# Hybrid encoder layer: gated output stored as VectorE's 32x32 blocks lie and placed at the loads; last step's loads in another order

## The chip, the core and the metric

One core of one Trainium2 chip runs the whole program. The metric is the device time in microseconds (us) of one execution. The engines are TensorE (PE; its weight loads are listed as PEld), VectorE (DVE), ScalarE (ACT), GpSimd (POOL) and SyncE (SP), which issues most of the transfers. Each engine runs its own instructions in order; between engines a semaphore makes one wait for another. All data are float32; matmuls that matter are split into a high and a low part, and three products of the parts are summed.

## The reference

One encoder layer on x (1, 2048, 1024). The input projection feeds two groups of heads; their outputs are joined and go through one output projection, with a residual and a layer norm:

```python
def hybrid_mixer(x, ...):
    (g_q, g_k, g_v, g_gate, g_lr_f, g_lr_b, m_cq, m_ckv, m_kr, m_gate) = jnp.split(x @ w_in, idx, axis=-1)
    o_a = gla_branch(...)   # (1, 2048, 512)
    o_b = mla_branch(...)   # (1, 2048, 512)
    return jnp.concatenate([o_a, o_b], axis=-1) @ w_out
# gla_branch ends:
    o = rms_norm(o_fwd + o_bwd, norm_g).reshape(B, S, D_GLA)
    return o * jax.nn.silu(gate)
# the layer:  x <- LayerNorm(alpha * x + hybrid_mixer(x))
```

`gla_branch` is a gated linear attention with 4 heads, forward and backward; `mla_branch` is a dense softmax attention with 4 heads and a gate. The change concerns the gated output of the first group, `o_a`, on its way to the output projection.

## The kernel before

The 2048 positions are 16 chunks of 128. The program has these stages, with their approximate place in the profiled execution:

- First sweep (0 to 340 us): the projections of the gated linear attention, chunk by chunk from the last. Each chunk's decayed queries, the intra-chunk output, the state and the gate go to scratch in DRAM (`qd_s`, `oi_s`, `su_s`, `u_s`).
- Second sweep (340 to 585 us): 16 chunks in 8 steps of 2. It loads a chunk's four scratch tensors, makes PE's product of queries and state (`Ob`), adds the intra-chunk output (`oib`), normalizes and gates (`og`), transposes on VectorE (`oT`) and stores the result to `oa_s`. In the same steps it does the projections of the second group: `ipm`, its norm `rm`, `cqT`, `pqr`, and the rope parts `qrTh`, `qrTl`, stored to `rh_s`, `rl_s`.
- Attention (580 to 1115 us): 16 blocks of a head and 512 queries. The first output chunks' loads are issued in its last blocks.
- Output projection (to the end): 16 chunks, each 48 matmuls, then residual and layer norm on VectorE, then two stores.

The order of the second sweep is written out as a table: `PLACE_C` gives each piece of work two places (for the first and the second chunk of a step, in units of steps), `PLACE_C_FIRST` and `PLACE_C_LAST` replace some of them for the first and the last step, and all pieces are sorted by place and then issued. `lS`, `lq`, `lo`, `lu` are the loads of `SU`, `qdb`, `oib` and `ub`; `lx` that of x. All of them are issued by SP, through `gl_load`, into tiles with two buffers each (three for `ub`). A load into a buffer that is in use waits on SP until the reader is done, and everything behind it in SP's order waits too.

`c_oT` (L1491) is VectorE's transpose: it turns each 32x32 block of the 128x512 tile in place and leaves the blocks where they are. A full transpose needs the blocks exchanged as well, within a head: before the change `c_soT` (L1493 to 1497) does that in the store, by four DMAs of 32 partitions, one for each block column, each in runs of 32 floats (128 bytes). `oa_s` then has the layout that the output projection needs, and `OutProj.load` (L1897) reads a chunk with one DMA, 128 rows of 2 KB.

`load` also fetches the chunk's gates (`gr`, two DMAs) and the second group's output (`of[:, 1]`). `load_res` (L1919) fetches `xr`, the residual of the chunk, 512 KB. In the loop over the chunks 4 to 15, ACT, POOL and SP follow the written order: split the loaded tensors of chunk c+2 into high and low parts, load chunk c+4, load the residual of c+1, product of c, finish of c (layer norm and stores). The loads end with chunk 15, so from the iteration of chunk 12 on there are none. `residual` (L1973) is VectorE's `rr = alpha * xr + product` and `finish` the norm. In between stand the last attention block's closing pieces: `tsum` (PE's `sx`, transposes of the softmax sums), `rcp` (VectorE's `rc`, L1677 and 1678) and `turn` (PE's `rt`, L1689). On PE and VectorE the order of the tail isn't written out but follows from a scheduler.

Of the kernel before, what the change touches and what calls it, by code (L numbers as in the profile page):

```python
# [9 lines left out]
F32 = mybir.dt.float32  # L10
# [8 lines left out]
P = 128  # L19
# [3 lines left out]
NCH = S // P  # L23
H = 4
# [63 lines left out]
    lo=(11.99, 11.22, 11.21, 12.62, 11.98, 11.51, 10.87, 10.63),  # L88
# [21 lines left out]
    lo=(15.35, 16.07, 20.38, 20.41, 24.45, 25.82, 33.5, 36.25),  # L110
# [55 lines left out]
    oT=(0.392, 1.103),  # L166
# [20 lines left out]
    lq=(-0.391, -0.03),  # L187
    lo=(-0.5, 0.357),
# [51 lines left out]
    oT=(0.805, 1.172),  # L240
# [20 lines left out]
    lq=(-1.8, 0.09),  # L261
    lo=(-0.452, -1.813),
# [37 lines left out]
    oT=(0.337, 0.509),  # L300
# [17 lines left out]
    vl=(0.968, 2.242),  # L318
    qrfa=(0.871, 2.029),
    lS=(-0.721, -0.203),  # L320
    lq=(-0.287, -0.357),
    lo=(-0.124, 0.045),
    lu=(0.281, 0.47),
    lx=(-0.48, -0.573),
    soT=(1.09, 2.304),
# [21 lines left out]
class K:  # L347
# [146 lines left out]
    def run(self):  # L494
        tc, nc, ins = self.tc, self.nc, self.ins
        with ExitStack() as top:
            cp = top.enter_context(tc.tile_pool(name="const", bufs=1))
            self.cp = cp
            dp = top.enter_context(tc.tile_pool(name="scr", bufs=1, space=DRAM))
# [4 lines left out]
            self.qa_s = [[dp.tile([P, H, QB], F32, name=f"q{p}_s{b}") for p in "hl"] for b in range(NQB)]  # L504
            self.qr_s = [[dp.tile([H, 64, QB], F32, name=f"r{p}_s{b}") for p in "hl"] for b in range(NQB)]
            self.gm_s = [dp.tile([P, H, QB], F32, name=f"gm_s{b}") for b in range(NQB)]
            self.oa_s = [dp.tile([P, H, P], F32, name=f"oa_s{c}") for c in range(NCH)]
            self.qk_s = [[dp.tile([64, H, P], F32, name=f"{n}_s{c}") for c in range(NCH)] for n in ("qx", "kx")]
            self.kt_s = [dp.tile([P, H, P], F32, name=f"kt_s{c}") for c in range(NCH)]
            self.r_s = [dp.tile([1, H, QB], F32, name=f"r_s{b}") for b in range(NQB)]  # L510
# [103 lines left out]
    def sweep_a(self):  # L614
        tc, nc, ins, cp = self.tc, self.nc, self.ins, self.cp
        with ExitStack() as ctx:
# [73 lines left out]
            def step(i, steps):  # L690

                def after(g, k):
                    for n, d, *count in steps.get((g, k), ()):
                        j = {"prev": i - 1, "cur": i, "next": i + 2}[d]
                        if n == "ld":
                            if j < NCH:
                                next(self.ga_ld(j))
                            elif j == NCH:
                                self.xb = self.load_x(NCH - 1, "xb")
                        elif n == "rope":  # L700
                            next(tables, None)
                        elif count:
                            some(n, j, *count)
                        elif (n, j) in begun:
                            for _ in begun.pop((n, j)):
                                pass
                        else:
                            run(n, j)
                for g in range(3):
                    for k in self.products(ch[i], g, after):  # L710
                        pass
                    after(g, NK - 1)
                if i and ch[i]["c"] not in LATE_GATES:
                    for k in self.gate_products(ch[i]["c"], *ch[i]["x"], ip):
                        after(3, k)
                    self.gate_end(ch[i]["c"], g1)

            self.first_lr = wdone[7][0]
            step(0, {(1, 5): [("lrT", "cur")]})
            ch[1]["x"] = self.split_x(xp, xnext, NCH - 2, "xa", "dve", 2)  # L720
            run("bst", 0)
            self.wgr = [self.wgp.tile([P, 512], F32, tag="wg", name=f"wgr{k}") for k in range(NK)]
            for k, raw in enumerate(self.wgr):
# [28 lines left out]
            with self.in_order(last):  # L752
                run("k", i)
                run("q", i)
# [347 lines left out]
    def late_gates(self):  # L1102
# [24 lines left out]
            self.Wz = next(wz)  # L1127
        self.tail = {e: self.merge(e, names) for e, names in zip(ENGINES[1:], (TAIL_ACT, TAIL_DVE))}

    def split_c(self, xf, j, eng="pool"):  # L1130
        self.hi(self.xch[:, :, j], xf)
        self.lo(self.xcl[:, :, j], xf, self.xch[:, :, j], eng)
# [358 lines left out]
        self.nc.vector.transpose(f2(d["oT"]), f2(d["og"]))  # L1491

    def c_soT(self, d):  # L1493
        t = d["oT"].rearrange("p h (a t) -> p h a t", a=4)
        dst = self.oa_s[d["c"]].rearrange("(a r) h (b t) -> b r h a t", a=4, b=4)
        for b in range(4):
            self.nc.sync.dma_start(dst[b], t[32 * b:32 * b + 32])

    def rope(self, dst, src, c, n):

# [37 lines left out]
    def attention(self):  # L1538
# [4 lines left out]
        with ExitStack() as ctx:  # L1543
# [269 lines left out]
            with fixed():  # L1813
                load(4)
                for c in (2, 3):
                    op.load_res(rest[c])
                load(5)
                split(4)
                load(6)
                op.load_res(rest[4])  # L1820
                for c in (0, 1):
                    op.finish(rest[c])
                split(5)
                load(7)
                op.load_res(rest[5])
                for c in (2, 3):
                    op.residual(rest[c], 0)
                    op.residual(rest[c], 1)
                    op.finish(rest[c])
# [16 lines left out]
class OutProj:  # L1846
# [39 lines left out]
    def load(self, o):  # L1886


        kern, nc, c = self.k, self.nc, o["c"]
        b, cs = c // 4, slice((c % 4) * P, (c % 4 + 1) * P)  # L1890
        of = o["of"] = kern.xfp.tile([P, 2, 4, P], F32, tag="xf", name=f"of{c}")
        if c < 4:
            gr = kern.xfp.tile([P, 2, 4, P], F32, tag="xf", name=f"gr{c}")
        else:
            gr = self.gr[c % 2] = self.gr.get(c % 2) or self.slot(f"gr{c}").rearrange("p a (b d) -> p a b d", b=4)
        o["gr"] = gr
        nc.sync.dma_start(of[:, 0], kern.oa_s[c])  # L1897
        nc.sync.dma_start(gr[:, 0], kern.gm_s[b][:, :, cs])
        nc.sync.dma_start(gr[:, 1], kern.r_s[b][:, :, cs].to_broadcast([P, 4, P]))
        nc.sync.dma_start(of[:, 1], kern.ob_s[b][:, :, cs])  # L1900
        o["oh"], o["ol"] = [], []
# [158 lines left out]
```

## Time and profile before

| | us |
|---|---|
| three runs | 1268.89, 1270.41, 1271.71 |
| median | 1270.41 |
| the profiled execution | 1270.53 |
| its span, first to last instruction | 1268.4 |
| PE busy in the span | 1247.2 (98%) |
| DVE busy | 893.5 (70%) |
| ACT busy | 727.9 (57%) |
| POOL busy | 718.6 (57%) |

The profiled execution's time is 2.13 us over its span. The mean granted TensorE clock is 0.997 of full speed. The profile's rows name a line of the kernel, an engine, an operation, and the output and inputs by the program's names. A number in brackets at the end of a row is the idle time just before it, with the engine or DMA that ended it; "us from issue to landing" is the time of a transfer from SP's instruction to its arrival.

### The profile page before, as it was taken

The numbers are of one execution on the slowest core, as the hardware profiler recorded it, in microseconds if no ns is written. First come the engines' busy times: TensorE is split into PE (matmuls) and PEld (weight loads), VectorE is DVE, ScalarE is ACT, GpSimd is POOL, SyncE is SP. The second block draws the span as 40 slices with busy tenths as digits, with TensorE's granted clock in tenths as the row PEclk, the third lists the DMA queues.
The fourth block names the chain that finished last, engine by engine and source line by source line (L and its number), as shares of the span: only waits on it lengthen the run. The fifth ranks groups of instructions, "written<-read, shape, count | busy, mean of one in ns | idle before, by whom it ended". The sixth has DMA issues, their size and how long they took to land.

```text
span 1268.4 us, 19649 instructions
## 1 busy us (share of the span) xinstructions
PE 1247.2 (98%) x6950; PEld 1100.2 (87%) x6950; DVE 893.5 (70%) x1610; ACT 727.9 (57%) x1177; POOL 718.6 (57%) x443
## 2 busy tenths in 40 slices
PE   8999999999999999989999999999999999999997
PEld 7999999999899999988788888888888888887886
DVE  6635555553665545564888888888888888389997
ACT  7544343454665444444888888888888888411110
POOL 0132323223265554430798888889999999935541
PEclk9999999999999999999999999999999999999999
DMA  8224555565857766747211111202133120376662
GB/s 297 76 82 124 136 144 137 144 134 159 274 173 211 210 187 204 211 133 199 76 32 53 40 45 42 59 9 59 58 92 92 42 42 26 122 231 195 208 191 100
DMA packets 188546, 160.10 MB, mean 126 GB/s; under 512 B 97206, under 2 KB 139838, under 8 KB 188448
## 3 DMA queue, kind: packets, MB, share of 16 engines
q1 hardware_dynamic: 180384, 156.72, 43.2%
q0 software_dynamic: 672, 2.10, 0.4%
q8 instruction: 55, 0.90, 0.3%
q10 hardware_dynamic: 7392, 0.03, 0.3%
q14 instruction: 43, 0.35, 0.1%
HBM read 102.79 MB, written 56.00 MB: 125 GB/s over the span
## 4 chain that ended last, share of the span: by engine, by line
PE 87%; issue 3%; DMA 3%; POOL 2%; DVE 2%; ACT 2%; SPq 1%; DVEq 0%; POOLq 0%; ACTq 0%
PE pz L1244 7%; PE ipm L1315 5%; PE o L412 5%; PE o L413 5%; PE o L414 4%; PE pS L1562 4%; PE pS L1563 4%; PE pS L1564 4%; PE pS L1565 4%; PE pS L1566 4%; PE ipa L412 4%; PE ipa L414 4%; PE ipa L413 4%; PE ipg L414 2%; PE ipg L413 2%
## 5 line engine op out<-in xcount | busy, mean ns | idle before, releaser
L364 POOL TENSOR_TENSOR pl<-s,ph 128x1024 fp32r<-128x1024 f32 x128 | 306.7, 2415 | 51.5 <-ACT ph L358 48.0
L1584 DVE TENSOR_TENSOR rm<-pS,rm 128x512 f32<-128x512 f32 x210 | 144.8, 690 | 36.3 <-ACT s L1571 30.7
L1571 ACT ACTIVATE s<-pS 128x1024 f32<-128x1024 f32 x128 | 131.2, 1025 | 61.3 <-PE pS L1566 51.7
L1608 DVE TENSOR_TENSOR s<-s,mb 128x1024 f32<-128x1024 f32 x128 | 151.2, 1213 | 8.9 <-PE mb L1602 8.2
L358 ACT ACTIVATE ph<-s 128x1024 fp32r<-128x1024 f32 x128 | 135.0, 1056 | 17.2 <-PE o L414 16.5
L1612 ACT ACTIVATE s<-s 128x1024 f32<-128x1024 f32 x128 | 131.4, 1049 | 9.4 <-DVE s L1608 9.3
L412 PE MATMUL ipa<-wah,xah 128*128 128x384 f32 (+1 forms) x384 | 128.8, 335 | 5.5 <-ACT wah L358 5.5
L413 PE MATMUL ipa<-wal,xah 128*128 128x384 f32 (+1 forms) x384 | 124.5, 324 | 0.0
L414 PE MATMUL ipa<-wah,xal 128*128 128x384 f32 (+1 forms) x384 | 124.5, 324 | 0.0
L1079 POOL TENSOR_TENSOR Sb<-Sb,Us 64x512 f32<-64x512 f32 x15 | 19.9, 1324 | 169.7 <-DVE Us L1071 160.6
L1562 PE MATMUL pS<-qh,ckvT_h 128*128 128x512 f32 x256 | 102.6, 401 | 0.8 <-DVE rm L1584 0.4
L412 PE MATMUL o<-ph,vh 128*128 128x512 f32 x256 | 101.1, 395 | 0.0
L1563 PE MATMUL pS<-ql,ckvT_h 128*128 128x512 f32 x256 | 100.0, 391 | 0.0
L1564 PE MATMUL pS<-qh,ckvT_l 128*128 128x512 f32 x256 | 99.9, 390 | 0.0
L1565 PE MATMUL pS<-rh,krs 128*128 128x512 f32 x256 | 99.9, 390 | 0.0
L1566 PE MATMUL pS<-rl,krs 128*128 128x512 f32 x256 | 99.8, 390 | 0.0
L414 PE MATMUL o<-ph,vl 128*128 128x512 f32 x256 | 99.8, 390 | 0.0
L413 PE MATMUL o<-pl,vh 128*128 128x512 f32 x256 | 99.7, 389 | 0.0
L1635 DVE TENSOR_TENSOR ap<-ap,s 128x512 f32<-128x512 f32 x120 | 83.0, 692 | 2.7 <-ACT s L1612 0.7
L412 PEld LDWEIGHTS ipa<-wah,xah 128*128 128x128 f32 x384 | 73.1, 190 | 8.4 <-ACT wah L358 5.5
L364 POOL TENSOR_TENSOR ol<-of,oh 128x512 fp32r<-128x512 f32 x32 | 43.0, 1344 | 64.3 <-ACT oh L358 64.3
L413 PEld LDWEIGHTS ipa<-wal,xah 128*128 128x128 f32 x384 | 73.2, 191 | 0.8 <-DVE wal L364 0.2
(302 smaller groups left out, 3427.3 us busy)
## 6 DMA issues: line engine op xcount, KB each, us to landing
xcf<-xT_dram SPq DMA_DIRECT2D x16, 512.0 KB, 5.4
xr<-x_dram SPq DMA_DIRECT2D x16, 512.0 KB, 6.3
out_dram<-rr SPq DMA_DIRECT2D x32, 256.0 KB, 2.1
xaf<-xT_dram SPq DMA_DIRECT2D x14, 512.0 KB, 4.2
oib<-oi_s SPq DMA_DIRECT2D x16, 256.0 KB, 3.7
qdb<-qd_s SPq DMA_DIRECT2D x16, 256.0 KB, 3.5
SU<-su_s SPq DMA_DIRECT2D x16, 256.0 KB, 3.9
ub<-u_s SPq DMA_DIRECT2D x16, 256.0 KB, 3.9
```

The source lines that it names most:

```text
L358: return nc.scalar.activation(dst, src, AF.Copy).ins
L364: return e.tensor_tensor(dst, src, hi.bitcast(F32), ALU.subtract).ins
L412: mm(out, ah, bh, start=start, stop=False)
L413: mm(out, ah, bl, start=False, stop=False)
L414: mm(out, al, bh, start=False, stop=stop)
L1562: mm(ps[:, e], kh, qh, start=True, stop=False)
L1563: mm(ps[:, e], kh, ql, start=False, stop=False)
L1564: mm(ps[:, e], kl, qh, start=False, stop=False)
L1565: mm(ps[:, e], kr, rh, start=False, stop=False)
L1566: mm(ps[:, e], kr, rl, start=False, stop=True)
L1584: V.tensor_tensor(d["rm"], src[:, e], d["rm"], ALU.max)
L1608: V.tensor_tensor(s, s, d["mb"][:, None, :].to_broadcast([P, 2, QB]), ALU.subtract)
```

## The change

Two things change. The gated output is stored by one DMA per chunk, with the 32x32 blocks where VectorE left them (`oa_s` becomes heads x partitions x columns), and the blocks are put in their places when the output projection loads them: four DMAs, one for each 32 partitions of the target, in runs of 128 bytes. And in the last step of the second sweep the places of the loads `lq` and `lo` are others.

```diff
@@ PLACE_C_LAST
     lS=(-0.721, -0.203),
-    lq=(-0.287, -0.357),
-    lo=(-0.124, 0.045),
+    lq=(-0.357, 0.05),
+    lo=(-0.14, 0.045),
     lu=(0.281, 0.47),
@@ scratch
-            self.oa_s = [dp.tile([P, H, P], F32, name=f"oa_s{c}") for c in range(NCH)]
+            self.oa_s = [dp.tile([H, P, P], F32, name=f"oa_s{c}") for c in range(NCH)]
+    def blocks_of(self, src):
+
+        v = src.rearrange("i (b r) m t -> m r (i b) t", b=4)
+        return [(slice(32 * m, 32 * m + 32), v[m]) for m in range(4)]
@@ c_soT
-        t = d["oT"].rearrange("p h (a t) -> p h a t", a=4)
-        dst = self.oa_s[d["c"]].rearrange("(a r) h (b t) -> b r h a t", a=4, b=4)
-        for b in range(4):
-            self.nc.sync.dma_start(dst[b], t[32 * b:32 * b + 32])
+        self.nc.sync.dma_start(self.oa_s[d["c"]].rearrange("h p f -> p h f"), d["oT"])
@@ OutProj.load
-        nc.sync.dma_start(of[:, 0], kern.oa_s[c])
+        for r, src in kern.blocks_of(kern.oa_s[c].rearrange("h p (m t) -> h p m t", t=32)):
+            nc.sync.dma_start(of[r, 0].rearrange("p h (b t) -> p (h b) t", t=32), src)
```

The first place is SP's order in the last step of the second sweep. The number in a name is the chunk (`qdb15` is chunk 15), for `rh`, `rl` the head group and step; the shape is the target's. Before:

```order
L1423 DMA ub13_6552<-u_s13_121 128x512
L1423 DMA qdb15_6555<-qd_s15_75 128x512
L1423 DMA qdb14_6572<-qd_s14_74 128x512
L1423 DMA SU15_6584<-su_s15_107 128x512
L1292 DMA rh_s2_136<-qrTh5_6320 128x256 x2
L1292 DMA rl_s2_137<-qrTl5_6321 128x256 x2
L1423 DMA oib14_6630<-oi_s14_90 128x512
L1423 DMA oib15_6692<-oi_s15_91 128x512
L1497 DMA oa_s12_156<-oT12_6421 128x4x32 x4
```

Now:

```order
L1428 DMA ub13_6516<-u_s13_121 128x512
L1428 DMA qdb14_6519<-qd_s14_74 128x512
L1428 DMA SU15_6546<-su_s15_107 128x512
L1428 DMA oib14_6582<-oi_s14_90 128x512
L1297 DMA rh_s2_136<-qrTh5_6287 128x256 x2
L1297 DMA rl_s2_137<-qrTl5_6288 128x256 x2
L1428 DMA oib15_6654<-oi_s15_91 128x512
L1428 DMA qdb15_6656<-qd_s15_75 128x512
L1499 DMA oa_s12_156<-oT12_6388 128x4x128
```

`qdb14` is now the first of the two, `qdb15` has moved behind `oib15`, `oib14` stands directly behind `SU15` and ahead of the four rope stores, and the store of `oa_s` is one row.

The second place is SP's order in the output projection, around one block of loads (chunk 9's, issued in the iteration of chunk 5; `xr6` is the residual of chunk 6). Before:

```order
L1989 DMA out_dram<-rr4_12056 128x512 x2
L1897 DMA of9_12122<-oa_s9_153 128x512
L1898 DMA gr5_11884<-gm_s2_142 128x4x128
L1899 DMA gr5_11884<-r_s2_210 128x4x128
L1900 DMA of9_12122<-ob_s2_214 128x4x128
L1919 DMA xr6_12127<-x_dram 128x1024
L1989 DMA out_dram<-rr5_12178 128x512 x2
```

Now:

```order
L1992 DMA out_dram<-rr4_12035 128x512 x2
L1900 DMA of9_12101<-oa_s9_153 32x16x32 x4
L1901 DMA gr5_11851<-gm_s2_142 128x4x128
L1902 DMA gr5_11851<-r_s2_210 128x4x128
L1903 DMA of9_12101<-ob_s2_214 128x4x128
L1922 DMA xr6_12109<-x_dram 128x1024
L1992 DMA out_dram<-rr5_12160 128x512 x2
```

The one row of `oa_s` has become four, ahead of the other loads and of `xr6`; the order is otherwise the same.

The third place is VectorE's reciprocal of the last attention block's sums (`rc15`), which the scheduler has moved. Before it stood behind chunk 5's residual:

```order
L1988 TENSOR_SCALAR rr4_12056<-rr4_12056,ln4_r_12094,lnb_11717 128x512 x2
L1973 TENSOR_SCALAR rr5_12178<-xr5_11961,po5_12129 128x512 x2
L1974 BN_STATS bn5_12179<-rr5_12178 128x6 x2
L1677 TENSOR_REDUCE rc15_12209<-sx15_12204 128x4
L1982 BN_AGGR mv5_12184<-bn5_12179 128x2
```

Now it stands in chunk 2's layer norm:

```order
L1986 TENSOR_SCALAR u2_11946<-mv2_11945 128x1
L1988 TENSOR_SCALAR rr2_11939<-rr2_11939,mv2_11945,lng_11680 128x512 x2
L1679 TENSOR_REDUCE rc15_12191<-sx15_12186 128x4
L1680 RECIPROCAL rc15_12191<-rc15_12191 128x4
L431 TENSOR_TENSOR ln2_t_11952<-ln2_y_11954,u2_11946 128x1
```

PE's transposes `sx15` that feed it have moved by about two chunks of matmuls as well. ACT's and POOL's order is the same as before.

## The prediction

> **What bounds the kernel now.** The page's head and its line of busy times come first.
>
> ```profile
> span 1268.4 us, 19649 instructions
> PE 1247.2 (98%) x6950; PEld 1100.2 (87%) x6950; DVE 893.5 (70%) x1610; ACT 727.9 (57%) x1177; POOL 718.6 (57%) x443
> ```
>
> TensorE (PE) is busy for 98% of the span, so a change that leaves its matmuls as they are can win only where PE stands still or runs at a lower clock. The next view, the table by stretches of time, says where that is. Its columns are the length, the busy time of PE, of its weight loads, of VectorE (DVE), ScalarE and GpSimd (POOL), the granted clock, the DMA share and GB/s. The rows are the middle of the second sweep, its last step, and the output projection.
>
> ```profile
> 500.00:540.00 40.00, 40.00 (x299) 39.12 (x299) 18.12 (x63) 18.74 (x49) 18.82 (x20) 1.00 0.68 203
> 540.00:580.00 40.00, 36.78 (x252) 34.45 (x251) 22.17 (x82) 17.27 (x56) 10.13 (x15) 0.96 0.54 147
> 1200.00:1240.00 40.00, 40.00 (x178) 33.12 (x178) 39.03 (x56) 6.25 (x16) 19.59 (x15) 1.00 0.56 178
> ```
>
> In the middle of the sweep PE has no gap. In the last step it loses 3.22 us of 40 and some clock besides. In the output projection PE is full, but DVE is too, at 39.03 of 40: there a delay of DVE has nowhere to go. The change touches just these two places.
>
> The next rows are the same table over 4 us each, with PE alone.
>
> ```profile
> 553.00:557.00 4.00, 1.38 (x6) 0.95 0.81 226
> 557.00:561.00 4.00, 3.71 (x17) 0.63 0.50 102
> ```
>
> Right after PE's longest gap the granted clock is 0.63 for 4 us. The stall costs its own length and then (1 − 0.63) × 4 = 1.48 and (1 − 0.95) × 4 = 0.2: 1.7 us of clock.
>
> The timeline of SyncE's queue (SPq) and its waits show what began that gap: the columns are start, length, line and transfer.
>
> ```profile
> 535.26 9.54 SPq L1423 DMA_DIRECT2D qdb<-qd_s  x2
> 544.89 0.74 SPq L1423 DMA_DIRECT2D SU<-su_s  x1
> 547.62 0.94 SPq L1423 DMA_DIRECT2D oib<-oi_s  x2
> SPq L1423 <- PE Ob L1462: 51.3, 9, 10.3
> ```
>
> SP issues in order. The second of the two qdb loads needs the buffer that PE's Ob of chunk 13 reads; SP stood 10.3 us before it (the last number, the longest of 9 waits). Behind it stand SU(15), four stores of two rope tensors, and only then oib(14), at 547.62. DVE and PE then wait for that transfer:
>
> ```profile
> 547.93 1.05 PE L1462 MATMUL Ob<-SU,qdb 128*128 128x128 f32 x8
> 551.40 0.70 DVE L1465 TENSOR_TENSOR Ob<-Ob,oib 128x512 f32<-128x512 f32 x1 [3.51 <-DMA oib<-oi_s]
> 555.82 0.42 DVE L364 TENSOR_TENSOR qrTl<-tq,qrTh 128x256 fp32r<-128x256 f32 x1
> 556.39 0.39 PE L412 MATMUL pqr<-wqr_h,cqT_h 128*128 128x256 f32 x1 [2.61 <-DVE rm_t L431]
> 557.29 0.58 PE L414 MATMUL pqr<-wqr_h,cqT_l 128*128 128x256 f32 x1 [0.30 <-DVE cqT_l L364]
> PEld pz L1244 <- DVE og L1485: 0.3, 1, 0.3
> ```
>
> DVE waits 3.51 us for oib, everything queued behind it on DVE is late by that, and PE's pqr waits 2.61 and 0.30 us for DVE.
>
> **The last step's loads: what it is worth.** The new order puts qdb(14) first, whose buffer is free early, and holds qdb(15) back to the end. SU(15) still waits for chunk 13's Ob, so SP is released at the same 544.4 (544.89 less the qdb issue of about 0.5). But oib(14) now stands directly behind SU(15): it goes out near 545.2 where it went out at 547.62, 2.4 us earlier. The add at 551.40 could then start at 549.0; PE's Ob(14), which ends at 547.93 + 1.05 = 548.98, is the other thing it needs and allows that too. DVE's chain moves up 2.4 us, so of the gaps of 2.61 and 0.30, about 0.5 stays: −2.4. If the gap is that short I take the clock dip as gone: −1.7. What is late next is the weight load that waits for og, 0.3 us now; I give back 0.2. **Sum −3.9 us.** Bounds: −2.2 if the dip stays, and 0 if SU(15) or a full DMA queue holds oib back as before. What qdb(15) loses by going last is covered: its Ob(15) runs one chunk later.
>
> On that dip the Trainium skill ("TensorE: Matmul & The Clock Gate", section "Part 1: The HAM clock gate (the "warmup" mystery)") says that the array falls to half clock after an idle window of about 3.4 us. Taken to the letter, a gap of 2.61 us would have no dip and the sum would be −2.2; the row with 0.63 shows a dip, and the measurement decides.
>
> **The store by one DMA instead of four.** It takes 48 issues from SP in the sweep:
>
> ```profile
> L1497 SPq DMA_DIRECT2D oa_s<-oT x64: 580/632/1392, 375.9 to 587.0; - x64
> 554.68 2.60 SPq L1497 DMA_DIRECT2D oa_s<-oT  x4
> L1897 SPq DMA_DIRECT2D of<-oa_s x16: 325/384/791, 940.7 to 1221.1; - x16
> ```
>
> Of the four issues' 2.60 us per chunk about 2 go. No engine waits for SP there but for the buffer wait above, and PE is full at 500 to 540, so I cost it at 0. The 0.2 in which the last stores of the step could help later loads is inside the error.
>
> **The load by four DMAs instead of one.** In the output projection each chunk's block of loads now issues four pieces of 32 partitions in 128-byte runs. The nearest row is the store of the same shape (x64 above, 632 ns; four of them 2.60 us) against 0.34 to 0.38 for the single load. So all that SP issues behind it, xr above all (the residual's 512 KB), goes out **δ = 2.60 − 0.34 = 2.3 us** later. From below: four pieces at the shortest issue of the loads, 325 ns, give δ = 1.0. From above: the landing of the small-run stores spreads to 5.5 where the median is 3.2, so the pieces may also hold the queue 2.3 us longer: δ = 4.6. I take 2.3, the row of the same shape.
>
> ```profile
> DMA to landing us min/median/max: 2.2/3.2/5.5
> ```
>
> Is there slack? xr(c+1) is issued behind the load of chunk c+4, which stands behind the stores of chunk c−1's result, which wait for DVE to finish chunk c−1. So a late DVE makes the next xr late, and δ comes on top once per two chunks. The rows are xr's issue with its landing, in the order of chunks 10, 12 and 13 (two more below), then the DVE instruction that needs each of chunks 2, 6, 8, 10, 12.
>
> ```profile
> L1919 SPq DMA_DIRECT2D xr<-x_dram x1: 617/617/617, 1202.1 to 1202.1; - x1
> DMA to landing us min/median/max: 7.2/7.2/7.2
> L1919 SPq DMA_DIRECT2D xr<-x_dram x1: 616/616/616, 1223.3 to 1223.3; - x1
> DMA to landing us min/median/max: 6.6/6.6/6.6
> L1919 SPq DMA_DIRECT2D xr<-x_dram x1: 424/424/424, 1242.3 to 1242.3; - x1
> DMA to landing us min/median/max: 3.6/3.6/3.6
> ```
>
> ```profile
> L1919 SPq DMA_DIRECT2D xr<-x_dram x1: 562/562/562, 1115.7 to 1115.7; - x1
> DMA to landing us min/median/max: 8.1/8.1/8.1
> L1919 SPq DMA_DIRECT2D xr<-x_dram x1: 868/868/868, 1160.7 to 1160.7; - x1
> xr<-x_dram SPq DMA_DIRECT2D x16, 512.0 KB, 6.3
> 1123.89 0.69 DVE L1973 SCALAR_TENSOR_TENSOR rr<-xr,pmb 128x512 f32<-128x512 f32 x1 [2.22 <-POOL of L1906]
> 1168.22 0.68 DVE L1973 SCALAR_TENSOR_TENSOR rr<-xr,pmb 128x512 f32<-128x512 f32 x1
> 1188.58 0.69 DVE L1973 SCALAR_TENSOR_TENSOR rr<-xr,pmb 128x512 f32<-128x512 f32 x1 [0.20 <-DMA xr<-x_dram]
> 1209.82 0.68 DVE L1973 SCALAR_TENSOR_TENSOR rr<-xr,pmb 128x512 f32<-128x512 f32 x1
> 1231.03 0.68 DVE L1973 SCALAR_TENSOR_TENSOR rr<-xr,pmb 128x512 f32<-128x512 f32 x1
> ```
>
> The slack of each is the start on DVE less issue plus landing. Chunk 2: 1123.89 − 1123.8, about 0. Chunk 6 (its landing taken at the page's median, 6.3): 1168.22 − 1167.0 = 1.2. Chunk 8 waits already: 0. Chunk 10: 1209.82 − 1209.3 = 0.5. Chunk 12: 1231.03 − 1229.9 = 1.1. With D as DVE's delay, D grows by 2.3 less the slack each time: 2.3, then 3.4, 5.7, 7.5, 8.7 at chunk 12. From the iteration of chunk 12 on no block is loaded, so xr of 13 to 15 takes no δ. At the end DVE has room, since it waits for PE there:
>
> ```profile
> 1257.53 0.42 DVE L1964 SCALAR_TENSOR_TENSOR rr<-xr,po 128x256 f32<-128x256 f32 x1 [1.46 <-PE po L414]
> 1260.40 0.42 DVE L1964 SCALAR_TENSOR_TENSOR rr<-xr,pap 128x256 f32<-128x256 f32 x1 [2.00 <-PE pap L414]
> ```
>
> That is 3.46 us. **Loss: 8.7 − 3.46 = 5.2 us**; in general 5δ − 2.8 − 3.46, at least 0.
>
> **The sums of the last attention block** move two chunks earlier on PE, and DVE makes their reciprocal earlier. This takes away one wait of PE:
>
> ```profile
> 1160.38 0.27 PE L1689 MATMUL rt<-ident,rc 128*4 128x128 f32 x1 [0.93 <-DVE rc L1677]
> ```
>
> While DVE sets the end, those 0.93 us only lengthen PE's later wait, so it is 0 here, and −0.93 where PE sets the end.
>
> **Sum:** −3.9 + 5.2 = +1.3 on the span of 1268.4: 1269.7. The profiled execution took 1270.53 us, 2.13 more than its span, so it becomes 1271.8. It lies 0.12 above the median of the runs, 1270.41; against that median I say **1271.7 us**. A measurement here can tell about 0.2% (2.5 us) from no change: faster ends at 1267.9, slower begins at 1272.95.
>
> **Rivals.**
> *The backlog swallows the delay (faster).* xr landed in 3.6 us at 1242.3, when no block was loaded, and in 6.6 to 8.1 behind one: most of its time is the queue ahead of it, so a later issue need not land later. With δ = 1.0, D is 1.0, 0.8, 1.8, 2.3, 2.2: under 3.46, no loss. Then PE sets the end, −3.9 − 0.93 = −4.8: 1265.6. Against it: DVE's 0.20 wait at 1188.58 shows xr with nothing to spare. Chance 0.25.
>
> *The small pieces land late (slower).* The 128-byte runs make 2048 packets per block of what were 2-KB rows, in the stretch with a DMA share of 0.56, and xr comes behind them on the same engines. With δ = 4.6: 5 × 4.6 − 6.26 = 16.7, less 3.9: +12.8, 1283.2. It makes the kernel slower by over 0.2% from 5δ − 6.26 − 3.9 = 2.5, δ = 2.5. For it: the spread of the landings of such stores. Against it: their median of 3.2 is no longer than that of larger transfers. Chance 0.28.
>
> The Trainium skill ("DMA: Bandwidth & Descriptors", section "🔬 Bandwidth") speaks for this rival: it calls transfers under 64 KB dominated by descriptors and gives 0.95 us for one of 64 KB. Four would be 3.8 us, an estimate from that page; with about 1 for the single load δ would be 2.9 and the sum +4.3. No run here shows such loads yet.
>
> *The stall stays (slower).* If SU(15) holds oib(14) back as qdb did, or oib lands no earlier through the backlog (DMA share 0.81 at 553), the gain is 0 and 5.2 remain: 1275.6. Chance 0.08.
>
> **How the numbers follow.** The forecast, most of the gain given back and a little more, has 0.39, with a range of its own of 1267.9 to 1274, of which 0.03 lies on the faster side, 0.22 within 0.2%, and 0.14 slower. Faster: 0.25 + 0.03 = 0.28. Same: 0.22. Slower: 0.28 + 0.08 + 0.14 = 0.50. The range reaches to the faster rival, 1265.5, and into the slower one up to 1280, δ = 4 (5 × 4 − 6.26 − 3.9 = 9.8); what is left out is the upper part of it and a gain over 4.9.
>
> **What would show it.** In the changed trace: PE's gap before pqr under 1 us and a clock of 1.00 at 553 to 561 (else the dip is not the gap's); SP's longest wait still before SU(15), with oib(14) right behind it; the four oa_s issues at about 2.6 us per block; DVE waiting for xr at chunks 2, 8 and 10, and less than 1.46 and 2.00 us for PE at the end. It is wrong if DVE waits for xr nowhere, or if ScalarE or POOL waits for the blocks themselves: I price their lateness at 0, since POOL is idle for half of 1200 to 1240 (19.59 of 40) and reads a block two chunks after its load.

## The result, and the profile after

The changed kernel takes 1268.35 us (median of 21 runs, 1266.51 to 1269.89) where the kernel before took 1270.71 (21 runs, 1268.89 to 1272.68). The ratio is 0.9982, with a 95% interval from 0.9976 to 0.9989: 2.4 us faster, just under the 0.2% that I took for the bound of a difference, but clear of no change. I had forecast 1271.7, a little slower. The profiled execution of the changed kernel took 1269.21 us, 0.86 over its median, and that of before 1270.53, 0.18 under its own; so a comparison of the two profiled executions shows 1.3 us of the 2.4.

The page of the changed kernel begins like this, the span and the busy time of each engine:

```profile
span 1267.4 us, 19686 instructions
PE 1246.5 (98%) x6950; PEld 1098.7 (87%) x6950; DVE 889.6 (70%) x1610; ACT 728.2 (57%) x1177; POOL 720.3 (57%) x443
```

The table by stretches (length, then PE, weight loads, DVE, ACT and POOL busy, granted clock, DMA share, GB/s) for the last step of the sweep and the output projection, and behind it the same with PE alone for the 8 us after the stall of before:

```profile
540.00:580.00 40.00, 38.43 (x275) 36.21 (x274) 23.34 (x87) 19.85 (x60) 11.58 (x17) 1.00 0.49 152
1200.00:1240.00 40.00, 40.00 (x178) 33.14 (x177) 37.42 (x53) 5.89 (x15) 17.97 (x14) 1.00 0.62 175
```

```profile
553.00:557.00 4.00, 2.62 (x13) 1.00 0.90 316
557.00:561.00 4.00, 3.85 (x31) 1.00 0.00 0
```

PE's busy time in the last step rises from 36.78 to 38.43 of 40, and the clock, which had averaged 0.63 over those 4 us, is 1.00. SyncE's timeline of that step and the instructions on DVE and PE that had waited:

```profile
535.47 1.16 SPq L1428 DMA_DIRECT2D qdb<-qd_s  x1
544.78 0.32 SPq L1428 DMA_DIRECT2D SU<-su_s  x1
545.14 1.06 SPq L1428 DMA_DIRECT2D oib<-oi_s  x1
549.29 0.70 DVE L1470 TENSOR_TENSOR Ob<-Ob,oib 128x512 f32<-128x512 f32 x1 [1.14 <-PE Ob L1467]
554.28 0.36 PE L412 MATMUL pqr<-wqr_h,cqT_h 128*128 128x256 f32 x1 [0.69 <-DVE rm_t L431]
555.19 0.38 PE L414 MATMUL pqr<-wqr_h,cqT_l 128*128 128x256 f32 x1 [0.44 <-DVE cqT_l L364]
557.15 0.67 PE L1320 MATMUL ipm<-wmh,xcl 128*128 128x448 f32 x2 [0.40 <-POOL xcl L364]
```

oib(14) goes out at 545.14 where it went out at 547.62. DVE's add now waits for PE and no longer for a transfer, and PE's gap before pqr is 0.69 + 0.44 us where it was 2.61 + 0.30. A wait of 0.40 for GpSimd is new.

The output projection has new waits. Rows of PE's, DVE's, SyncE's and GpSimd's timelines:

```profile
1148.91 0.50 PE L412 MATMUL pmb<-woh,oh 128*128 128x512 f32 x1 [0.37 <-ACT oh L358]
1150.78 0.50 PE L414 MATMUL pmb<-woh,ol 128*128 128x512 f32 x1 [1.14 <-POOL ol L364]
1173.08 0.27 PE L1691 MATMUL rt<-ident,rc 128*4 128x128 f32 x1 [1.14 <-ACT rt L1697]
1122.79 0.69 DVE L1976 SCALAR_TENSOR_TENSOR rr<-xr,pmb 128x512 f32<-128x512 f32 x1 [3.18 <-DMA xr<-x_dram]
1200.52 1.28 DVE L1976 SCALAR_TENSOR_TENSOR rr<-xr,po 128x512 f32<-128x512 f32 x2 [1.79 <-DMA xr<-x_dram]
1222.94 1.28 DVE L1976 SCALAR_TENSOR_TENSOR rr<-xr,po 128x512 f32<-128x512 f32 x2 [1.37 <-DMA xr<-x_dram]
1259.39 0.42 DVE L1967 SCALAR_TENSOR_TENSOR rr<-xr,pap 128x256 f32<-128x256 f32 x1 [0.99 <-PE pap L414]
1222.03 2.05 SPq L1900 DMA_DIRECT2D of<-oa_s  x4
1116.22 4.52 SPq L1900 DMA_DIRECT2D of<-oa_s  x4
1130.47 3.15 POOL L1909 TENSOR_TENSOR of<-of,gr 128x512 f32<-128x512 f32 x2 [2.50 <-DMA of<-ob_s]
```

The four pieces take SyncE 1.91 to 2.06 us in 11 of the 16 blocks, and more in the pieces before the loop: 4.52, 3.46 and 2.97 us for chunks 5, 6 and 7, where the single load took 0.57, 0.33 and 0.41. DVE waits for xr at chunk 2 (3.18 us; before, it waited 2.22 there, for GpSimd) and at chunks 9 and 11. GpSimd waits 2.50 us for chunk 5's block itself, which it did not before. DVE's room at the end shrinks from 3.46 to 0.99 us. It is not used up: PE still sets the end. PE itself waits 2.65 us (0.37 + 1.14 + 1.14) in this stage where it waited 1.41.

To place gains and losses I cut each trace at two of PE's instructions that all kernels have. The first is the first `Op` that waits for DVE at the end of the first sweep, the second the first `mx` of the attention, and the end is PE's last matmul. For the two kernels these rows are:

```profile
335.85 1.16 PE L1054 MATMUL Op<-V,At 128*128 128x128 f32 x8 [0.58 <-DVE At L1047]
603.68 0.66 PE L1590 MATMUL mx<-ident,rm 128*128 128x128 f32 x4 [0.31 <-DVE rm L1584]
1260.09 0.28 PE L414 MATMUL pap<-woh,ol 128*128 128x256 f32 x1
```

```profile
336.10 1.16 PE L1054 MATMUL Op<-V,At 128*128 128x128 f32 x8 [0.58 <-DVE At L1047]
601.03 0.66 PE L1592 MATMUL mx<-ident,rm 128*128 128x128 f32 x4 [0.31 <-DVE rm L1586]
1259.07 0.28 PE L414 MATMUL pap<-woh,ol 128*128 128x256 f32 x1
```

The stretch with the last step (A) went from 267.83 to 264.93, a gain of 2.90 us. The rest, with the output projection (B), went from 656.41 to 658.04, a loss of 1.63. The same cuts in all profiled executions, with each kernel's median and its ratio to the kernel before in the same job (95% interval):

| kernel | A | B | median, us | ratio |
|---|---|---|---|---|
| before | 267.83 | 656.41 | 1270.71 | |
| the change | 264.93 | 658.04 | 1268.35 | 0.9982 (0.9976 to 0.9989) |
| e1 places alone | 265.92 | 656.30 | 1268.60 | 0.9981 (0.9972 to 0.9990) |
| e2 layout alone | 269.82 | 656.95 | 1272.76 | 1.0018 (1.0009 to 1.0027) |
| e3 places, load in 4 x 32 rows | 265.55 | 659.52 | 1269.53 | 0.9991 (0.9980 to 1.0002) |
| e4 change, residual first in the loop | 265.02 | 656.27 | 1267.90 | 0.9978 (0.9968 to 0.9987) |
| e5 only lq | 266.95 | 654.73 | 1269.89 | 0.9994 (0.9984 to 1.0003) |
| e6 only lo | 266.45 | 655.62 | 1268.15 | 0.9984 (0.9975 to 0.9993) |
| e7 change, blocks not placed | 264.96 | 655.00 | 1267.17 | 0.9975 (0.9967 to 0.9984) |
| e8 change, residual first everywhere | 264.97 | 655.49 | 1267.22 | 0.9973 (0.9963 to 0.9983) |
| e9 change, 8 pieces | 264.96 | 667.66 | 1279.19 | 1.0067 (1.0050 to 1.0083) |
| e10 change, pieces from ScalarE | 264.94 | 669.11 | 1277.84 | 1.0063 (1.0044 to 1.0082) |
| e11 e1, residual first everywhere | 266.02 | 656.73 | 1269.33 | 0.9988 (0.9979 to 0.9996) |

A is steady: the six profiles that share the change's store and places (the change, e4, e7, e8, e9, e10) lie between 264.93 and 265.02. B is one execution each and less steady: before, e1, e5 and e6 have the same instructions in the same order in the output projection and lie between 654.73 and 656.41. Most of that spread is PE's waits for rc and rt (1.41 us in the kernel before, 1.57 in e1, 0.49 in e6, none to be seen in e5). The kernel before is at the upper end, and the profiled executions of e5 (1268.18) and e10 (1282.18) are the fastest and the slowest run of theirs. So a difference of 1 us or so in B has to be read together with the medians.

The kernels also differ in what the scheduler made of the tail. PE's and VectorE's order in the output projection is that of the kernel before in e1, e5, e6 and e7, and PE's in e3, e10 and e11 too. The earlier sums of the last attention block (`sx`, `rc`, and with them one `rt`) stand in the change and in e2, on PE also in e4 and nearly so in e9; e8 has an order of its own. PE's row of the sums in the change and in e7:

```profile
1123.24 0.60 PE L1673 MATMUL sx<-ident,acc 128*128 128x128 f32 x4
```

```profile
1146.07 0.60 PE L1673 MATMUL sx<-ident,acc 128*128 128x128 f32 x4
```

So a comparison of B across these groups is one of two orders as well as of two ways to load. No run has the change's loads with the order of before on SyncE, PE and VectorE.

### The profile page after: what moved, and what is told of

Same layout as the page of the kernel before. It is cut to its first block, busy times and chain, and to the rows that moved or that the text cites. A ratio compares the mean times of both kernels' runs of the same rounds, so it can differ in the third digit from the quotient of the medians.

```text
span 1267.4 us, 19686 instructions
## 1 busy us (share of the span) xinstructions
PE 1246.5 (98%) x6950; PEld 1098.7 (87%) x6950; DVE 889.6 (70%) x1610; ACT 728.2 (57%) x1177; POOL 720.3 (57%) x443
## 4 chain that ended last, share of the span: by engine, by line
PE 88%; DMA 3%; DVE 2%; issue 2%; ACT 2%; POOL 1%; SPq 1%; DVEq 0%; POOLq 0%; ACTq 0%
PE pz L1249 7%; PE ipm L1320 5%; PE o L412 5%; PE o L413 5%; PE o L414 5%; PE pS L1564 4%; PE pS L1566 4%; PE pS L1567 4%; PE pS L1568 4%; PE pS L1565 4%; PE ipa L412 4%; PE ipa L414 4%; PE ipa L413 4%; PE ipg L414 2%; PE ipg L412 2%; PE ipg L413 2%
```

## The experiments

**e1: the last step's places alone** (kernel before, with the change's two lines of the table).

```diff
-    lq=(-0.287, -0.357),
-    lo=(-0.124, 0.045),
+    lq=(-0.357, 0.05),
+    lo=(-0.14, 0.045),
```

> The kernel before with only the last step's load places of the change; store and loads of oa_s as before. Theory A (the two edits act apart: the last step gains about 2.9 us, the four-piece loads cost 1.2 to 1.6 us in the output projection): this part alone gains the whole 2.9 us or a little more, 1267.2 to 1268.0 beside a before of 1270.7, so it is at least as fast as the change; in the trace PE's gap before pqr is about 1.1 us with a clock of 1.00 at 553 to 561, and DVE's room at the end stays near 3.5 us less what PE came earlier. Theory B (the output projection takes the gain back whatever the loads look like, since VectorE and SyncE there come no earlier when PE does): 1269.0 to 1270, slower than the change, with new PE waits between 1140 and 1180.

Measured: 1268.60, and neither theory as it was put. B shows no loss (656.30), so the output projection does not take the gain back by itself: theory B falls. But A gained only 1.91 us where the change gained 2.90. The trace says why. Its rows on DVE, PE and SyncE:

```profile
557.25 1.13 DVE L1485 SCALAR_TENSOR_TENSOR og<-Ob,rg_r,ub 128x128 f32<-128x128 f32 x4 [1.23 <-DMA ub<-u_s]
564.45 0.39 PE L1244 MATMUL pz<-xch,wzh 128*128 128x256 f32 x1 [0.90 <-DVE og L1485]
549.31 2.73 SPq L1497 DMA_DIRECT2D oa_s<-oT  x4
552.78 0.62 SPq L1423 DMA_DIRECT2D ub<-u_s  x1
```

With oib(14) early, the next in line is the gate tensor ub: its load stands behind the four store DMAs of chunk 12 and goes out at 552.78; DVE waits 1.23 us for it and PE 0.90 for DVE. In the changed kernel the store is one DMA, ub goes out at 550.30, and both waits are gone:

```profile
549.21 0.48 SPq L1499 DMA_DIRECT2D oa_s<-oT  x1
550.30 0.73 SPq L1428 DMA_DIRECT2D ub<-u_s  x1
```

So the store is worth 1.0 us in A once the places are new.

**e2: the layout alone** (the change, with the two lines of the table as before).

```diff
-    lq=(-0.357, 0.05),
-    lo=(-0.14, 0.045),
+    lq=(-0.287, -0.357),
+    lo=(-0.124, 0.045),
```

> The change with the last step's load places of before: only the store of one DMA and the four-piece loads. Theory A: the last step keeps its stall of 2.6 us and its clock dip, and the loads cost 0.5 to 1.6 us: 1271.2 to 1272.3 beside a before of 1270.7. Theory B: the loads cost nothing of their own, 1270.0 to 1271.0. My prediction's sum had +5.2, which would be 1275.9.

Measured: 1272.76, ratio 1.0018: slower than before, and beyond the bounds of both theories. B is longer by only 0.54; most is in A, 1.99 us. With the old places SyncE gets to oib(14) 0.44 us later than before (548.06), DVE's add starts 0.9 us later, and PE's gap is 3.09 us where it was 2.61. The dip of the clock behind it is longer. DVE's row:

```profile
552.28 0.70 DVE L1470 TENSOR_TENSOR Ob<-Ob,oib 128x512 f32<-128x512 f32 x1 [4.35 <-DMA oib<-oi_s]
```

The stretches of 4 us behind that gap, PE alone:

```profile
557.00:561.00 4.00, 3.58 (x11) 0.51 0.35 97
561.00:565.00 4.00, 4.00 (x23) 0.64 0.00 0
```

(0.49 + 0.36) x 4 = 3.4 us of clock, against 1.7 before. The same store that gains 1.0 us with the new places goes with a loss of 2.0 with the old ones. What makes oib land later, the store's own earlier issue or the loads behind it, was not separated.

**e3: the pieces without the small runs** (places of the change; store as before; four loads of 32 whole rows).

```diff
-        nc.sync.dma_start(of[:, 0], kern.oa_s[c])
+        for m in range(4):
+            r = slice(32 * m, 32 * m + 32)
+            nc.sync.dma_start(of[r, 0], kern.oa_s[c][r])
```

> The kernel before with the last step's new places, and each block of oa_s loaded by four DMAs of 32 whole rows (2-KB runs) where there was one DMA: the count of the change's issues without its small runs. If it is the count of issues on SyncE that costs (each about 0.4 to 0.5 us, so xr goes out 1.2 to 1.6 us later), it is as fast as the change or up to 0.5 us faster, 1267.8 to 1268.5. If it is the 128-byte runs, their packets and their landing, it is as fast as the places alone, 1267.2 to 1268.0 with DVE's waits for xr back under 0.5 us.

Measured: 1269.53, with 0.9991 (0.9980 to 1.0002), outside both ranges. It is not as fast as the places alone by the medians, and DVE's waits for xr are there, 3.30, 1.51 and 0.27 us at chunks 2, 6 and 9; that speaks for the count of issues (1.80 us for four on SyncE's timeline, at 1159.34, nearly the 2.05 of the small runs; 416 ns for one in the median, where the small runs take 487). But its runs fall in two groups, 1268.49 to 1269.53 and 1271.31 to 1273.30, and the profiled one is of the upper group. In it PE waits 1.91 us for DVE's rc (before rt, which is a wait of 0.93 in the kernel before), and the clock drops behind that gap, which was not expected. The stretches at the gap:

```profile
1156.00:1160.00 4.00, 2.22 (x10) 1.00 0.54 174
1160.00:1164.00 4.00, 3.87 (x11) 0.57 0.49 139
```

That the dip makes the upper group is likely (0.43 x 4 = 1.7 us), but only one run of it was profiled. The median of the lower group is 1268.9, only 0.3 above e1; if that group has no dip, the four issues cost next to nothing without it.

**e4: the residual ahead of the block, in the loop** (the change otherwise).

```diff
-                    load(c + 4)
                     if 4 < c < NCH - 1:
                         op.load_res(rest[c + 1])
+                    load(c + 4)
```

> The change with the residual's load of chunk c+1 issued ahead of the block of chunk c+4 instead of behind it, in the loop over the chunks 5 to 14; all else the same. Theory A with xr as the carrier (the four pieces delay xr, xr delays VectorE): DVE's waits for xr of 1.79 and 1.37 us at chunks 9 and 11 go, its room at the end grows from 0.99 back to above 2 us; the time falls only by what PE still waits, 0.3 to 1.2 us, to 1267.1 to 1268.1. If the carrier is the block itself (ScalarE and GpSimd split chunk 6 late, PE waits 1.5 us for it before the loop's residuals matter), the two PE waits stay, and the time is within 0.4 us of the change or a little longer, since the blocks go out later still.

Measured: 1267.90, inside the first range. DVE's waits for xr at chunks 9 and 11 are gone, and B is 656.27, the level of the kernel before, with PE's order of the change; so the earlier sums need not cost anything. At the very end DVE waits only 1.44 us for PE and not above 2, but it waits 3.82 us for it already at chunk 14. PE's wait for chunk 6 stays, smaller, at 0.78 us. DVE still waits 2.28 us for chunk 2's xr in the pieces before the loop, where the order was left as it was; e8 changes it there.

**e5 and e6: one load at a time** (kernel before, with only lq's or only lo's new places).

```diff
 e5
-    lq=(-0.287, -0.357),
+    lq=(-0.357, 0.05),
 e6
-    lo=(-0.124, 0.045),
+    lo=(-0.14, 0.045),
```

For lq alone:

> The kernel before with only lq's new places: qdb(14) first and qdb(15) last, oib(14) still behind SU(15) and the four rope stores. If the gain of the last step comes from the blocked qdb alone, the stall goes as in the change and the time is that of the places together, 1268.6. By my reading it does not: SyncE still waits for chunk 13's Ob, now at SU(15), and oib(14) goes out only about 0.5 us earlier than before (547.1 for 547.6), so PE's gap before pqr stays above 2 us and the time is 1269.8 to 1270.8.

For lo alone:

> The kernel before with only lo's new places: oib(14) directly behind SU(15) and ahead of the rope stores, the two qdb in their old order. By my reading this carries most of the gain: oib(14) goes out near 545.6, 2 us earlier than before, PE's gap before pqr falls to about 1 us, the clock stays at 1.00, and the time is 1268.4 to 1269.2. If the blocked qdb carries it, the stall stays and the time is that of before, 1270.9.

Measured: lq alone 1269.89 (0.9994, 0.9984 to 1.0003), lo alone 1268.15. The times came as read, lo alone a little faster. With lq alone the 10 us block is gone from qdb, but SyncE stands before SU(15) instead; oib(14) goes out at 547.48 (said: 547.1), PE's gap is 2.29 and the clock falls still. With lo alone qdb blocks as before, and oib(14) goes out at 546.48, 0.9 later than I had said; PE has 1.40 us of gap earlier (for GpSimd's qrf) and then 0.59 + 0.44, at a clock of 1.00. The first fence is e5's (the stretch from 557 to 561 with its clock), the other two e6's (the transfer on SyncE's timeline, and the same stretch):

```profile
557.00:561.00 4.00, 4.00 (x23) 0.73 0.40 91
```

```profile
546.48 0.42 SPq L1423 DMA_DIRECT2D oib<-oi_s  x1
```

```profile
557.00:561.00 4.00, 3.60 (x25) 1.00 0.47 104
```

The gain of the last step comes mostly from oib's place ahead of the rope stores, not from the blocked qdb: in A lo alone gains 1.38 us and lq alone 0.88 where both gain 1.91, and by the medians lo alone is as fast as both together. How it gains is not quite what I had read. PE's waits in the last step add up to 3.16 us before, 2.83 with lo alone, 2.29 with lq alone and 2.45 with both. With lo alone they are hardly shorter, but no single gap is long, and the dip of the clock is gone; with lq alone the waits are shorter and the dip stays.

**e7: the blocks not put in their places** (the change with one DMA per block of loads; the first group's part of the output is permuted).

```diff
-        for r, src in kern.blocks_of(kern.oa_s[c].rearrange("h p (m t) -> h p m t", t=32)):
-            nc.sync.dma_start(of[r, 0].rearrange("p h (b t) -> p (h b) t", t=32), src)
+        nc.sync.dma_start(of[:, 0], kern.oa_s[c].rearrange("h p f -> p h f"))
```

> The change with each chunk's oa_s loaded by one DMA in the stored order, so that the blocks are not put in their places and the first group's part of the output is permuted: the work of the four-piece loads is left out, the store of one DMA and the last step's places stay. Theory A (the store is worth about 1 us in the last step because ub(14) gets out behind it earlier; the four-piece loads cost 0.6 to 1.6 us in the output projection): 1266.8 to 1267.7, faster than the change by 0.6 to 1.6 us and than the places alone by about 1. Theory B (the loads cost nothing that stays): 1268.1 to 1268.6 as the change.

Measured: 1267.17, theory A's range. A is the change's (264.96), B is 655.00, and PE's waits for chunk 6's split are gone. So the four-piece loads, with the order that the scheduler makes for them, do cost: 1268.35 − 1267.17 = 1.2 us by the medians, 3 us by the two profiles. (The way over e1 gives less: the change is 0.25 us faster than e1 and gains 1.0 more in A, which leaves 0.7 for the loads.) e7 has the order of the kernel before on PE and VectorE, so it does not part the loads from the moved sums. A way of the loads to PE can be followed by comparing the two traces. In the changed kernel:

```profile
1132.74 2.95 SPq L1992 DMA_DIRECT2D out_dram<-rr  x4
1139.28 1.28 DVE L1976 SCALAR_TENSOR_TENSOR rr<-xr,po 128x512 f32<-128x512 f32 x2 [1.59 <-DMA out_dram<-rr]
1143.12 0.20 ACT L425 ACTIVATE ln_l<-u 128x1 f32<-128x1 f32 x1 [8.51 <-DVE u L1986]
1148.23 0.63 ACT L358 ACTIVATE oh<-of 128x512 fp32r<-128x512 f32 x1 [4.08 <-POOL of L1909]
```

and in e7, the same four:

```profile
1129.53 3.36 SPq L1991 DMA_DIRECT2D out_dram<-rr  x4
1136.06 1.28 DVE L1975 SCALAR_TENSOR_TENSOR rr<-xr,po 128x512 f32<-128x512 f32 x2
1139.94 0.20 ACT L425 ACTIVATE ln_l<-u 128x1 f32<-128x1 f32 x1 [6.88 <-DVE u L1985]
1145.06 0.63 ACT L358 ACTIVATE oh<-of 128x512 fp32r<-128x512 f32 x1 [4.16 <-POOL of L1908]
```

Ahead of the first stores of results SyncE issues two blocks of loads; in pieces, these push the stores from 1129.53 to 1132.74. DVE waits 1.59 us for a buffer that those stores free, ScalarE's norm waits for DVE, chunk 6's split stands behind the norm on ScalarE (the row shows its second half, which stands behind GpSimd's part of the first), and comes 3.2 us later; PE waits 0.37 and 1.14 us for it. The moved reciprocal is not what sets this: it stands on DVE at 1134.10, ahead of the wait of 1.59 us, whose end the stores set. PE's other wait, 1.14 us for rt, is 0.41 in e7, 1.13 in e2 and 0.67 in e4, which have the change's order on PE, and 0.20 to 0.49 in e1, e3, e6, e7 and e11, which have the old one. That wait may come of the order as well as of the loads; it was not separated. (By mx, e7's trace runs 1.07 us later than the change's, so each of these delays is 1 us more.)

**e8: the residual first, before the loop too** (e4's edit, and this).

```diff
-                load(4)
                 for c in (2, 3):
                     op.load_res(rest[c])
+                load(4)
                 load(5)
                 split(4)
-                load(6)
                 op.load_res(rest[4])
+                load(6)
...
-                load(7)
                 op.load_res(rest[5])
+                load(7)
```

> The change with the residual ahead of the block as in e4, and in the pieces before the loop too: residuals 2 and 3 ahead of block 4, residual 4 ahead of block 6, residual 5 ahead of block 7. If xr's lateness in that stretch (DVE waits 1.09 and 2.28 us there in e4) is what makes PE wait for chunk 6's split and for the rt copy, both waits shrink and the time is 1266.8 to 1267.6. If the blocks themselves are late, PE's wait for GpSimd's ol grows by up to the 1 us that two residuals take to issue, and the time is that of e4 or up to 1 us more, 1267.9 to 1268.9.

Measured: 1267.22, ratio 0.9973, inside the first range: PE's wait in chunk 6 is gone, rt waits 0.24, and B is 655.49. The scheduler's order on PE and VectorE is another here as well. This is a version that beats both kernels: 1.1 us under the change by the medians, though single runs of the two overlap (1266.51 to 1268.39 here).

**e9: eight pieces of 16 partitions instead of four of 32.**

```diff
-            nc.sync.dma_start(of[r, 0].rearrange("p h (b t) -> p (h b) t", t=32), src)
+            for q in range(2):
+                s = slice(r.start + 16 * q, r.start + 16 * q + 16)
+                nc.sync.dma_start(of[s, 0].rearrange("p h (b t) -> p (h b) t", t=32), src[16 * q:16 * q + 16])
```

> The change with each block of oa_s loaded by eight DMAs of 16 partitions instead of four of 32: the same bytes and runs, twice the issues on SyncE. In the change four take 2.04 us against 0.38 for the one, so xr goes out 1.65 us later; eight should make it about 3.7 us. By the chain of my prediction (each second chunk adds the delay less the slack: 5 x 3.7 - 6.26 = 12 us lost against 2.0 by the same formula for four) the time is 1276 to 1280, with DVE waiting for xr at nearly every second chunk and no room at the end. If the loss is only PE's two waits for late blocks and does not add up from chunk to chunk, it is 1269 to 1271.

Measured: 1279.19, in the range of the chain. The eight take 3.77 us in the row below (others longer, up to 7.25), so the delay is at least 3.77 − 0.38 = 3.4 us, and 5 x 3.4 − 6.26 = 10.7; B is longer by 11.25. But it does not come out where I had it: PE waits 3.59 us for DVE's rr in mid-projection, after DVE waited 6.24 for xr, and the clock of that stretch is 0.91 (the second fence, by stretches), (1 − 0.91) x 40 = 3.6 us; with 0.96 in the 40 us before it, 1.6 more. The formula knows no clock, so 5.2 of the 11.25 us are not its own, and DVE still waits 1.47 us for PE at the end. That the totals agree is luck; that the loss grows much faster than the number of pieces is shown.

```profile
1188.66 3.77 SPq L1902 DMA_DIRECT2D of<-oa_s  x8
1177.89 0.69 DVE L1978 SCALAR_TENSOR_TENSOR rr<-xr,pmb 128x512 f32<-128x512 f32 x1 [6.24 <-DMA xr<-x_dram]
```

```profile
1160.00:1200.00 40.00, 36.41 (x150) 29.27 (x149) 29.59 (x44) 6.17 (x16) 17.61 (x13) 0.91 0.69 185
```

**e10: the pieces issued by ScalarE.**

```diff
-            nc.sync.dma_start(of[r, 0].rearrange("p h (b t) -> p (h b) t", t=32), src)
+            nc.scalar.dma_start(of[r, 0].rearrange("p h (b t) -> p (h b) t", t=32), src)
```

> The change with the four pieces of each block issued from ScalarE's queue instead of SyncE's; runs, packets and bytes the same. If SyncE's serial issue is the carrier of the loss (the four pieces ahead of xr and of the stores), the loss goes as it went where the blocks were not placed: 1266.9 to 1267.7. If the small runs' packets on the DMA engines are the carrier, the time stays that of the change, 1268.0 to 1268.7. ScalarE has room for the issues in the output projection, but pieces of chunks 0 to 3 are issued in the attention, where they may cost up to 0.5 us.

Measured: 1277.84 (six runs, 1275.23 to 1282.18; the profiled one is the slowest). Both expectations missed: the issue blocks the queue that it stands in, and ScalarE's own work is behind it. In the attention ScalarE stands 5.26 us, which gives PE a gap of 3.37 us; DVE waits 6 us twice for xr in the projection. So it tells nothing for or against SyncE as the carrier; e9 and e4 speak for it, as does e7 within its limits. In the row of the queue and the one of the engine:

```profile
1030.67 6.16 ACTq L1900 DMA_DIRECT2D of<-oa_s  x4
1036.87 1.06 ACT L1614 ACTIVATE s<-s 128x1024 f32<-128x1024 f32 x1 [5.26 <-DMA gr<-gm_s]
```

**e11: e8's order with the old layout** (e1, with the two edits of e4 and e8).

> The kernel before with the last step's new places and the residuals ahead of the blocks as in e8, but with the store of four DMAs and the load of one. If e8 is fast because of the residuals' order alone, this is as fast or faster, 1266.6 to 1267.3, since its loads are cheaper still. If the one-DMA store is worth its 1 us in the last step and the four-piece loads cost nothing once the residuals go first, it is slower than e8 by 0.5 to 1.2 us: 1267.7 to 1268.5, with PE waiting 0.9 us for og there.

Measured: 1269.33, slower than e8 by 2.1 us by the medians, more than the 1.2 that the second reading allowed, and outside both ranges. In A it is e1 again (266.02, with PE's 0.90 us wait for og), 1.05 behind e8; B is 656.73 against 655.49. It is no faster than e1 either (1268.60): the order alone gains nothing there. So of e8's lead 1.05 us is the one-DMA store, in A; the rest, in B, was not separated from the scheduler's order on PE and VectorE, which differs between the two.

## Why the prediction was wrong

**The step that failed is the loss of 5.2 us in the output projection**, "5δ − 2.8 − 3.46" with δ = 2.3. The runs show about 1 us by the medians (1.2 against e7, 0.7 by way of e1) and 1.6 between the two profiled executions. Two things in the step were wrong.

The first is the size of δ: "I take 2.3, the row of the same shape". Four loads in the loop take SyncE 2.05 us, not 2.60: δ = 2.05 − 0.38 = 1.65, in most blocks. That row belonged to stores of the same shape, and a load of it issues faster: 487 ns in the median, in the tile's row of the changed kernel, where the stores took 632.

```profile
L1900 SPq DMA_DIRECT2D of<-oa_s x64: 302/487/2041, 937.8 to 1223.6; - x64
```

Each 0.1 us of δ counts five times: with 1.65 the same formula gives 5 x 1.65 − 6.26 = 2.0 us where I had 5.2, and −3.9 + 2.0 would have been a forecast of 1.9 us faster. That this lies near the measured 2.4 would be luck, since the second thing is the path. The formula lets DVE set the end, and DVE does not: 0.99 us of its room is left, and in e9, at δ = 3.4, 1.47. The Trainium skill's table ("DMA: Bandwidth & Descriptors", section "🔬 Bandwidth") had led to an estimate of 2.9 for δ, further off; the measured issue decides. (That estimate took about 1 us for the single load of 256 KB, a size that the table has no row for.)

**The mechanism of the loss was half right.** The pieces delay what SyncE issues behind them, and DVE waits for xr: at chunk 2 (3.18 us), as I had named, and at 9 and 11 (1.79 and 1.37 us) where I had named 8 and 10. The loss reached PE elsewhere, as its waits for chunk 6's split and for rt: the first through the delayed stores of results, DVE's buffers and ScalarE's order, the second through ScalarE and perhaps the moved sums. The blocks of chunks 5 to 7, before the loop, where the pieces took up to 4.52 us, are not in the formula at all. I had priced the lateness of the split at 0, because GpSimd was half idle. GpSimd and ScalarE do wait for chunk 5's block itself (2.50 and 1.00 us), which I had named as a sign of being wrong; chunk 6's split, which PE waits for, is late because of what stands ahead of it on ScalarE, not for want of time.

**The sums of the last attention block** were put at 0, and at −0.93 where PE sets the end. PE does set the end and the wait of 0.93 for rc is gone, but the next rt waits 1.14 us for ScalarE where it waited 0.48. The 0.93 is no fixed price either: with the order of before, rt waits 1.09 us for rc in e1, 0.79 in e11, 1.91 in e3, and not at all in e5, e6 and e7.

**The last step's loads: mechanism right, 2 us too much.** oib(14) went out at 545.14 (said: 545.2), the add started at 549.29 (549.0), and the dip went. I had −3.9; the places alone gave −1.9 in A. The gap fell to 1.13 us and not to 0.5, the next wait, put at 0.2, was 0.90 (og, through ub), and one of 0.42 came at the next ipm product. The prediction told lq's and lo's moves as one; lo's carries most of it (e5, e6).

**The store was not free.** "I cost it at 0" was wrong by 1.0 us: it removes the next wait in the last step, since SyncE gets to ub 2.5 us earlier. It is worth that only with the new places.

**The sum**, by the cuts: −1.9 for the places, −1.0 for the store, +1.6 for the loads, −1.3 in the profiled executions, and −2.4 in the medians. The forecast had −3.9, 0 and +5.2. The rival in which the backlog swallows the delay is in part borne out: xr at chunks 10 and 12 landed in 6.8 and 5.7 us where it had taken 7.2 and 6.6. The rival in which the small pieces land late is not: a piece landed 2.7 us after its issue in the median, the single load of before 2.9. (The row at 1242.3, given to chunk 13 in the prediction, is chunk 14's xr; nothing hangs on it.)

## What to carry to other kernels

When a delay is repeated along a chain, its size per turn is the number to get right, and a row of the same shape in the other direction is no price for it; bound it by the row of the load as well as of the store before taking either. Ask, too, at each turn which engine sets the end: here it was PE all along, and VectorE's lateness counted only where PE came to wait for it. On an engine that issues in order, ask for each wait removed which instruction of the same queue is late next: here the earlier load was worth 1.9 us, and the shorter store behind it another 1.0, which alone, with the old order, came with a loss. A load that must come in pieces goes behind what is waited for soonest: with that order the change was 1.1 us faster by the medians. And where a scheduler writes part of the order, compare its order before comparing times: leaving out one edit here changed another engine's order as well.

## What was not expected of the hardware

The granted clock falls after gaps of PE shorter than I would have thought, and what a dip costs comes in steps. After a gap of 2.29 us (e5) the clock was 0.84 and 0.73 in two stretches of 4 us from about its start, after 2.61 (before) 0.95 and 0.63, after 1.91 (e3) 0.57 in one stretch. By what is missing to 1.00, times 4 us, each of these is 1.7 us. After 3.09 (e2) it was 0.51 and 0.64, 3.4 us, twice as much. The length of the gap alone does not say which: in e10 a gap of 3.37 us (in the attention) was followed by 0.93, 0.50 and 0.72, 3.4 us, and one of 3.93 (at 1182) by 0.85 and 0.72, 1.7 us. After 1.40 us (e6), after 0.69 + 0.44 and after 1.14 (the change) the clock stays at 1.00; but in e9 two gaps close together, 1.15 and 0.62 us, were followed by 0.77 and 0.80, again 1.7 us. So in these runs every single gap of 1.91 us or more brought a dip and none up to 1.40 did; where between them it begins was not measured. The Trainium skill ("TensorE: Matmul & The Clock Gate", section "Part 1: The HAM clock gate (the "warmup" mystery)") speaks of an idle window of about 3.4 us; most of the dips here come after shorter gaps.
